# The chunk scan of an SSD layer in two halves traced one step apart, with TensorE in program order in the group loop

## The chip, the cores and the metric

The kernel runs on one NeuronCore of a Trainium2 chip. The metric is the device time of one execution, in microseconds (us), from the first to the last instruction. Its engines each take their instructions in order: TensorE (PE, with the weight loads on PEld), VectorE (DVE), ScalarE (ACT), GpSimd (POOL) and SyncE (SP), whose queue issues nearly all DMAs. Matmuls write to PSUM banks of 128 x 512 numbers; tiles for the other engines are in SBUF.

## The reference

One inference step of two layers, a Mamba-2 SSD layer and an MLA attention layer, for a prompt of 1024 tokens and 8 samples of 8 tokens each. The change is in the SSD layer. Per group g of 8 (4 heads of 64 columns, a state of 128):

```python
proj = jnp.einsum('btd,de->bte', h, w_in)                 # z, x, B, C, dt
xbc = jax.nn.silu(causal_conv(xbc, ...))                  # x, B, C
seg = a_cs[..., :, None] - a_cs[..., None, :]             # chunks of 128 tokens
decay = jnp.where(causal, jnp.exp(jnp.where(causal, seg, 0.0)), 0.0)
cb = jnp.einsum('bclgn,bcsgn->bgcls', cc, bc)
y_diag = jnp.einsum('bgrcls,bcsgrp->bclgrp', cb[:, :, None] * decay, xdt)
states = jnp.einsum('bcsgn,bcsgrp->bcgrpn', bc, xdt * decay_end[..., None])
# S[c+1] = chunk_decay * S[c] + states[c];  y_off = (C S) * decay_in
y = (y_diag + y_off + d_skip * xs) * silu(z)
yg = yg * rsqrt(mean(yg * yg) + eps)                      # per group
out = jnp.einsum('bte,ed->btd', yg * norm_w, w_out)
```

The prompt is 8 such chunks in series. Every sample has a recurrent state of its own that is read from memory, used in y_off, updated and written back.

## The kernel before

Products in float32 are made of three products of high and low halves (`split`: a cast on ScalarE, then a subtraction on DVE or POOL). Group 0's projections come first. Then a loop over g = 0 to 6 runs the scan of group g (`ssd_scan`, a generator) beside the projections of group g + 1 (`Group.steps`): after every yield as many projection pieces are traced as the yielded weights add up to, 21 a group. A piece is 24 matmuls: 12 pieces "pj" of 128 x 384 or 128 x 320 with the convolution's input, 9 pieces "pz" of 128 x 256 for the gate z (the last of them 16 matmuls for the 64 sample rows). The last scan (g = 7) runs beside the first half of the output projection (poa); its second half (pob) and the MLA layer follow and are left as they are.

What is traced in this order is then put in order by the framework's scheduler on every engine, TensorE's too: it takes whatever it expects to be ready first. A tile's buffers are taken in turn: a tile name with two buffers lets the third tile start only when the first one's last reader is done. The PSUM banks are tr 2, pj 2, cb 1, y 2, st 1.

A step of `ssd_scan` is one chunk of 128 tokens (i = 0 to 7), the ninth (i = 8) the 64 sample rows. The names in the profile:
- trp: transposes of x and B into the tr bank; xsT, xdt, xdd and BT come from it. xdd is split into xddh and xddl.
- cb: the product of B and C in the cb bank; cbm: the same with the mask.
- M: the cumulated log decays are read by a DMA (acs_d) into M; subtraction and minimum with 0 on DVE (L575), Exp on ScalarE (L577), product with cbm on DVE (L578).
- py: M with xdt in one half of the y bank (L582), C with the split state S in the other; st: the chunk's own state.
- y: sum, times z, squares summed (L662), times the norm weight nw on POOL (L663), written to y_d.
- For the samples: four tiles s0 with 4 sample states each for two heads (256 KB, two buffers), read (L628), transposed (s0p, L631), split (sh, sl), multiplied with C into pv, which lies in the cb bank (L640), decayed on POOL (L641), sn (L644) added on DVE (L646), written (L647). x3p, x3, b3 and bb are the operands of sn, for two of the four tiles at a time. yo collects pv on ScalarE and DVE (L652, L653).
- wraw, wih, wil: a projection weight as loaded (L272) and its two halves (L129 on ScalarE, L130 on DVE); woh, wol: the halves of w_out (L703, L704), wol by turns on DVE and POOL.
- ahead of the loop `ssd_dt` turns the last columns of the projection into dt, with softplus on ScalarE, and cumulates with the matmuls dpa, dpt, acsp and decp; acs_d is written from that.

Of the kernel before, what the change touches and what calls it, by code (L numbers as in the profile page):

```python
# [405 lines left out]
class Group:  # L406
# [10 lines left out]
    def pair(self, pi, both=False):  # L417
# [3 lines left out]
        if both:  # L421
            for _ in range(3):
# [98 lines left out]
def ssd_scan(k, gr, pools):  # L521
    nc, I = k.nc, k.I
    sp, psum = pools
    g = gr.g
    S = None
    hs = slice(4 * g, 4 * g + 4)
    nw = sp.tile([128, 256], F32, tag="nw", name=f"nw{g}", bufs=1)
    nc.sync.dma_start(nw, I["ssd_norm_w"][0, 256 * g : 256 * g + 256].partition_broadcast(128))
    for i in ORDER[g]:
        t0, m = TILES[i]  # L530
        sl = slice(t0, t0 + m)
        smp = i == 8
        B, C, X0, X1 = (gr.xc[q][1][:, j] if smp else gr.xc[q][0][:, j, sl] for q in range(2) for j in range(2))
        z = gr.z[i // 5][:m, i % 5]
        tag = f"{g}_{i}"
        p = psum.tile([128, 512], F32, tag="tr", name="trp" + tag, bufs=PB["tr"])
        nc.tensor.transpose(p[:m, 0:128], X0, k.ident)
        nc.tensor.transpose(p[:m, 128:256], X1, k.ident)
        if not smp:
            nc.tensor.transpose(p[:m, 256:384], B, k.ident)  # L540
        xsT = sp.tile([128, 256], F32, tag="xsT", name="xsT" + tag, bufs=2)
        nc.scalar.copy(xsT[:m], p[:m, 0:256])
        if not smp:
            Bh, Bl = (sp.tile([128, 128], F32R, tag="BT" + x, name="BT" + x + tag, bufs=2) for x in "hl")
            split(k, Bh, Bl, p[:, 256:384])
        tk = k.tok[:m, i]

        def hb(j):
            return tk[:, j, hs].unsqueeze(2).to_broadcast([m, 4, 64])

        def v3(t):
            return t[:m].rearrange("p (h q) -> p h q", q=64)

# [20 lines left out]
        for h in range(4):  # L574
            nc.vector.tensor_scalar(M[:m, h, :m], M[:m, h, :m], tk[:, 0, 4 * g + h : 4 * g + h + 1], 0.0,  # L575
                                    op0=ALU.subtract, op1=ALU.min)
# [1316 lines left out]
```

## Time and profile before

| | |
|---|---|
| median of 3 runs | 2095.51 us (2094.92 to 2098.74) |
| profiled execution, span | 2095.4 us |
| mean granted clock of TensorE | 0.969 |
| start and group 0's projections | 0 to 133 us |
| group loop, g = 0 to 6 | 133 to 848 us, some 104 us a group |
| last scan with poa | 848 to 1017 us |
| pob | 1017 to 1125 us |
| MLA layer | 1125 to 2095 us |

The profile is of one execution. Busy time is given for each engine; for matmuls, which overlap, the busy time of a stretch is the time in which at least one was running. A row of the timeline has the start, the duration, the engine, the line and the operation, then output and operands, and in brackets how long the engine stood idle before it and what ended that. A row of the stretches has the length, the busy time (and instructions) of PE, PEld, DVE, ACT and POOL, the granted clock (1.00 is full speed), the share of DMA engines and GB/s. A row of waits has the sum, the number of times and the longest.

### The profile page before, as it was taken

The numbers are of one execution on the slowest core, as the hardware profiler recorded it, in microseconds if no ns is written. First come the engines' busy times: TensorE is split into PE (matmuls) and PEld (weight loads), VectorE is DVE, ScalarE is ACT, GpSimd is POOL, SyncE is SP. The second block draws the span as 40 slices with busy tenths as digits, with TensorE's granted clock in tenths as the row PEclk, the third lists the DMA queues.
The fourth block names the chain that finished last, engine by engine and source line by source line (L and its number), as shares of the span: only waits on it lengthen the run. The fifth ranks groups of instructions, "written<-read, shape, count | busy, mean of one in ns | idle before, by whom it ended". The sixth has DMA issues, their size and how long they took to land.

```text
span 2095.4 us, 33766 instructions
## 1 busy us (share of the span) xinstructions
PE 1948.3 (93%) x12001; PEld 1763.6 (84%) x12001; DVE 1340.1 (64%) x2838; ACT 1043.3 (50%) x2287; POOL 851.9 (41%) x1059
## 2 busy tenths in 40 slices
PE   6999999999999999789998999699999999889998
PEld 5898999899999998677787998698888888778887
DVE  4558676767676767865334314366787778776665
ACT  5455565556565656522114323234676667755552
POOL 0337564646664646744000001102343334765541
PEclk9999999999999999889999999899999989999999
DMA  4222324231324241635534342132111112464451
GB/s 144 56 59 64 111 66 115 56 114 57 105 66 115 56 115 46 208 122 192 183 124 133 124 152 63 52 108 68 48 55 52 43 37 61 133 197 131 142 152 40
DMA packets 187631, 207.61 MB, mean 99 GB/s; under 512 B 23260, under 2 KB 153064, under 8 KB 187080
## 3 DMA queue, kind: packets, MB, share of 16 engines
q1 hardware_dynamic: 182408, 185.67, 29.2%
q0 software_dynamic: 4976, 19.66, 3.0%
q8 instruction: 95, 1.56, 0.3%
q14 instruction: 72, 0.59, 0.1%
q10 hardware_dynamic: 80, 0.13, 0.0%
HBM read 152.10 MB, written 53.28 MB: 98 GB/s over the span
## 4 chain that ended last, share of the span: by engine, by line
PE 33%; DVE 9%; issue 4%; POOL 4%; DMA 3%; ACT 2%; SPq 0%; POOLq 0%; DVEq 0%; ACTq 0%
PE pq L100 5%; PE pob L100 5%; PE pj L88 4%; PE poa L100 2%; POOL kvl L1541 2%; PE pk L100 1%; PE p L100 1%; PE vp L88 1%; PE st L1246 1%; DVE tl L1260 1%; PE st L1248 1%; PE st L1247 1%; PE o L1277 1%; PE sc L1214 1%; PE kp L88 1%
## 5 line engine op out<-in xcount | busy, mean ns | idle before, releaser
L88 PE MATMUL pj<-xh,wih 128*128 128x384 f32 (+1 forms) x768 | 254.9, 336 | 10.9 <-ACT xh L235 6.6
L88 PE MATMUL pj<-xl,wih 128*128 128x384 f32 (+1 forms) x768 | 255.9, 333 | 0.0
L88 PE MATMUL pj<-xh,wil 128*128 128x384 f32 (+1 forms) x768 | 255.1, 332 | 0.0
L1260 POOL TENSOR_TENSOR tl<-P,th 128x384 fp32r<-128x384 f32 (+1 forms) x96 | 90.7, 945 | 181.0 <-ACT P L1258 138.5
L88 PEld LDWEIGHTS pj<-xh,wih 128*128 128x128 f32 x768 | 145.8, 191 | 12.5 <-ACT xh L235 7.5
L468 DVE SCALAR_TENSOR_TENSOR acc<-raw,vec,acc 128x1112 f32<-128x1112 f32 x96 | 147.0, 1535 | 11.9 <-ACT acc L465 11.1
L88 PEld LDWEIGHTS pj<-xh,wil 128*128 128x128 f32 x768 | 146.3, 190 | 0.6
L88 PEld LDWEIGHTS pj<-xl,wih 128*128 128x128 f32 x768 | 146.1, 190 | 0.5
L575 DVE TENSOR_SCALAR M<-M,tok 128x128 f32<-128x128 f32 (+1 forms) x288 | 116.6, 462 | 43.0 <-DMA M<-acs_d 35.7
L100 PE MATMUL pz<-wih,xh 128*128 128x256 f32 x504 | 143.0, 287 | 0.0
L100 PE MATMUL pz<-wil,xh 128*128 128x256 f32 (+1 forms) x504 | 142.8, 287 | 0.0
L1257 ACT ACTIVATE th<-st 128x512 fp32r<-128x512 f32 x192 | 94.1, 490 | 73.6 <-PE st L1253 54.7
L100 PE MATMUL pz<-wih,xl 128*128 128x256 f32 x448 | 128.1, 286 | 0.0
L130 DVE TENSOR_TENSOR wil<-wraw,wih 128x512 fp32r<-128x512 f32 x88 | 70.4, 802 | 65.7 <-ACT wih L129 63.1
L1541 POOL TENSOR_TENSOR kvl<-pgr,kvh 128x1024 fp32r<-128x1024 f32 x32 | 78.2, 2445 | 67.8 <-ACT kvh L1540 67.8
L100 PEld LDWEIGHTS pz<-wih,xh 128*128 128x128 f32 x504 | 96.0, 190 | 1.1
L577 ACT ACTIVATE M<-M 128x512 f32<-128x512 f32 (+1 forms) x72 | 43.8, 608 | 102.0 <-DVE M L575 101.7
L1258 ACT ACTIVATE P<-st 128x512 f32<-128x512 f32 x192 | 93.2, 486 | 0.0
L100 PEld LDWEIGHTS pz<-wil,xh 128*128 128x128 f32 (+1 forms) x504 | 92.9, 184 | 0.3
L663 POOL TENSOR_TENSOR y<-y,nw 128x256 f32<-128x256 f32 (+1 forms) x72 | 64.5, 896 | 70.2 <-ACT xD L662 69.7
L582 PEld LDWEIGHTS py<-xdt,M 128*128 128x128 f32 (+1 forms) x576 | 70.4, 192 | 19.8 <-DVE xdt L555 6.5
L100 PEld LDWEIGHTS pz<-wih,xl 128*128 128x128 f32 x448 | 85.4, 191 | 0.4
(819 smaller groups left out, 6461.6 us busy)
## 6 DMA issues: line engine op xcount, KB each, us to landing
wraw<-in_ssd_w_in SPq DMA_DIRECT2D x92, 256.0 KB
M<-acs_d SPq DMA_DIRECT2D x64, 256.0 KB
s<-in_state_ssm SPq DMA_DIRECT2D x32, 256.0 KB
y_d<-y SPq DMA_DIRECT2D x64, 128.0 KB
out_s_ssm<-s SPq DMA_DIRECT2D x32, 256.0 KB
wraw<-in_ssd_w_out SPq DMA_DIRECT2D x16, 512.0 KB
q_d<-qt SPq DMA_DIRECT2D x32, 192.0 KB
qp<-q_d SPq DMA_DIRECT2D x8, 768.0 KB
```

Of the source, the lines that this page charges most:

```text
L88: nc.tensor.matmul(out, a, b, start=(i == 0), stop=(i == n - 1))
L100: nc.tensor.matmul(o, a, b, start=(j == 0), stop=(j == len(ops) - 1))
L130: (eng or nc.vector).tensor_tensor(lo, src, hi.bitcast(F32), op=ALU.subtract)
L468: nc.vector.scalar_tensor_tensor(acc, raw[:, j : j + n], k.convw[j][:, blk : blk + 1], acc, op0=ALU.mult, op1=ALU.add)
L575: nc.vector.tensor_scalar(M[:m, h, :m], M[:m, h, :m], tk[:, 0, 4 * g + h : 4 * g + h + 1], 0.0, op0=ALU.subtract, op1=ALU.min)
L577: nc.scalar.activation(M[:m, :, :m], M[:m, :, :m], AF.Exp)
L582: nc.tensor.matmul(py[:m, h * 64 : h * 64 + 64], M[:m, h, :m], xdt[:m, h * 64 : h * 64 + 64], start=True, stop=True)
L663: nc.gpsimd.tensor_tensor(y[:m], y[:m], nw[:m], op=ALU.mult)
L1257: nc.scalar.activation(th[:, :n], ps[:, :n], AF.Exp, scale=SCALE)
L1258: nc.scalar.activation(P[:, :n], ps[:, :n], AF.Exp, scale=SCALE)
L1260: eng.tensor_tensor(tl[:, :n], P[:, :n], th[:, :n].bitcast(F32), op=ALU.subtract)
L1541: nc.gpsimd.tensor_tensor(rl, raw, rh.bitcast(F32), op=ALU.subtract)
```

## The change

1. The generator `ssd_scan` becomes a class `Scan`. A chunk is done by `front(i)` (read of M, trp, xdt, xdd, cb, the decay in M) and `back(i)` (st, py, the update of S, the splits of the new S and of the next chunk's C, y). front(i + 1) is traced ahead of back(i), with yields after each: 17 yields of 15/17 for the chunks and five of 6/5 for the samples. The samples' work is cut into `turn_state(n)` (read of s0, s0p, split), `use_state(n)` (pv, decay, sn, write) and `triples(q)` (x3p to bb); turn_state(n + 1) is traced ahead of use_state(n). Buffers: M 3 (2 before), xddh and xddl 2 (1), xsT 1 (2), y 1 (2); s0 stays at 2.
2. The loop over the groups stands under `tc.manual_schedule` for TensorE: its instructions keep the order in which they are traced. The other engines are scheduled as before, and so are the start and the last scan.
3. The decay is four Relu on ScalarE (scale -1, bias the row's own value), then Exp with scale -1, in place of the four subtractions on DVE.
4. The norm weight is multiplied into w_out: woh is made by ScalarE with it as a scale, wol by a scalar_tensor_tensor on DVE for all 16 blocks. The product on POOL and the DMA of nw are gone.
5. The Silu of both column pairs of a group stand behind the second pair.

TensorE has 11581 matmul instructions in both; DVE goes from 2840 to 2560, ACT from 2123 to 2439 (288 Relu, and 78 table loads in place of 50), POOL from 1064 to 984, SP from 843 to 835.

```diff
         xs = self.ap.tile([128, 2, NB * NT], F32, tag=f"xs{pi}", name=f"xs{g}{pi}", bufs=1)
-        nc.scalar.activation(acc[:, :, :SEQ], acc[:, :, :SEQ], AF.Silu)
-        nc.scalar.activation(xs.rearrange("p a (b w) -> p a b w", w=NT),
-                             bass_window(acc, SEQ + 3, NT + 3, NT), AF.Silu)
         self.xc.append((acc, xs))
         if pi:
+            for acc, xs in self.xc:
+                nc.scalar.activation(acc[:, :, :SEQ], acc[:, :, :SEQ], AF.Silu)
+                nc.scalar.activation(xs.rearrange("p a (b w) -> p a b w", w=NT),
+                                     bass_window(acc, SEQ + 3, NT + 3, NT), AF.Silu)
...
-def ssd_scan(k, gr, pools):
...
+class Scan:
...
+    def front(self, i):
...
+        M = c.M = self.tile([128, 4, 128], "M", "M" + tag, 3)
+        nc.sync.dma_start(M[:m, :, :m], (k.acss_d[hs] if smp else k.acs_d[i, hs]).partition_broadcast(m))
+        p = self.bank("tr", "trp" + tag)
+        nc.tensor.transpose(p[:m, 0:128], c.X0, k.ident)
+        nc.tensor.transpose(p[:m, 128:256], c.X1, k.ident)
...
+        xsT = self.tile([128, 256], "xsT", "xsT" + tag, 1)
         nc.scalar.copy(xsT[:m], p[:m, 0:256])
...
+        xdt = c.xdt = self.tile([128, 256], "xdt", "xdt" + tag, 2)
+        nc.vector.tensor_tensor(c.v3(xdt), c.v3(p[:, 0:256]), c.hb(1), op=ALU.mult)
...
+            c.Bh, c.Bl = (self.tile([128, 128], "BT" + x, "BT" + x + tag, 2, F32R) for x in "hl")
+            split(k, c.Bh, c.Bl, p[:, 256:384])
+            c.dh, c.dl = (self.tile([128, 256], "xdd" + x, "xdd" + x + tag, 2, F32R) for x in "hl")
+            xdd = self.tile([128, 256], "xdd", "xdd" + tag, 1)
+            nc.gpsimd.tensor_tensor(c.v3(xdd), c.v3(xsT), c.hb(2), op=ALU.mult)
+            split(k, c.dh, c.dl, xdd, nc.gpsimd)
...
+        pc = self.bank("cb", "cb" + tag)
+        nc.tensor.matmul(pc[:m, :m], c.B, c.C, start=True, stop=True)
+        cbm = self.tile([128, 128], "cbm", "cbm" + tag, 1)
         nc.vector.tensor_tensor(cbm[:m, :m], pc[:m, :m], (k.masks if smp else k.masku)[:m, :m], op=ALU.mult)
-        M = sp.tile([128, 4, 128], F32, tag="M", name="M" + tag, bufs=2)
-        nc.sync.dma_start(M[:m, :, :m], (k.acss_d[hs] if smp else k.acs_d[i, hs]).partition_broadcast(m))
         for h in range(4):
-            nc.vector.tensor_scalar(M[:m, h, :m], M[:m, h, :m], tk[:, 0, 4 * g + h : 4 * g + h + 1], 0.0,
-                                    op0=ALU.subtract, op1=ALU.min)
-        nc.scalar.activation(M[:m, :, :m], M[:m, :, :m], AF.Exp)
+            nc.scalar.activation(M[:m, h, :m], M[:m, h, :m], AF.Relu, bias=tk[:, 0, 4 * g + h : 4 * g + h + 1], scale=-1.0)
+        nc.scalar.activation(M[:m, :, :m], M[:m, :, :m], AF.Exp, scale=-1.0)
         nc.vector.tensor_tensor(M[:m, :, :m], M[:m, :, :m],
                                 cbm[:m, :m].unsqueeze(1).to_broadcast([m, 4, m]), op=ALU.mult)
-        py = psum.tile([128, 512], F32, tag="y", name="py" + tag, bufs=PB["y"])
+        return c
...
+    def back(self, c, nxt):
+        k, nc, i, hs, tag = self.k, self.k.nc, c.i, self.hs, c.tag
+        ps = self.bank("st", "st" + tag)
+        py = self.bank("y", "py" + tag)
+        mm3(nc, ps[:, :256], [(c.Bh, c.dh), (c.Bh, c.dl), (c.Bl, c.dh)])
+        self.within(c, py)
+        S, S2 = self.S, self.tile([128, 256], "S", f"S{self.g}_{i + 1}", 2)
+        if S is None:
+            nc.vector.tensor_copy(S2, ps[:, :256])
         else:
+            Sh, Sl = self.split_S
+            mm3(nc, py[:, 256:], [(c.Ch, Sh), (c.Ch, Sl), (c.Cl, Sh)])
+            nc.gpsimd.tensor_tensor(S2.rearrange("p (h q) -> p h q", q=64), S.rearrange("p (h q) -> p h q", q=64),
+                                    k.decp[:, hs, i : i + 1].to_broadcast([128, 4, 64]), op=ALU.mult)
+            nc.vector.tensor_tensor(S2, S2, ps[:, :256], op=ALU.add)
+        self.S = S2
+        if i < 7:
+            Sh, Sl = self.split_S = [self.tile([128, 256], "S" + x, "S" + x + tag, 1, F32R) for x in "hl"]
+            split(k, Sh, Sl, S2, nc.gpsimd)
+            nxt.Ch, nxt.Cl = (self.tile([128, 128], "C" + x, "C" + x + tag, 1, F32R) for x in "hl")
+            split(k, nxt.Ch, nxt.Cl, nxt.C, nc.gpsimd)
+        self.out(c, py, py[:, 256:] if i else None)
+
...
+    def out(self, c, py, off):
...
         nc.vector.tensor_tensor(y[:m], y[:m], z, op=ALU.mult)
-        nc.scalar.activation(xD[:m], y[:m], AF.Square, accum_out=k.yssq[:m, i, g : g + 1])
-        nc.gpsimd.tensor_tensor(y[:m], y[:m], nw[:m], op=ALU.mult)
-        nc.sync.dma_start(k.y_d[sl, 256 * g : 256 * g + 256], y[:m])
+        nc.scalar.activation(c.xD[:m], y[:m], AF.Square, accum_out=k.yssq[:m, i, g : g + 1])
+        nc.sync.dma_start(k.y_d[c.sl, 256 * g : 256 * g + 256], y[:m])
...
+    def triples(self, c, q):
+        k, nc, tag, hs = self.k, self.k.nc, c.tag, self.hs
+        p = self.bank("tr", f"x3p{tag}{q}")
+        xr = self.tile([128, 4, 128], "M", f"xr3{tag}{q}", 3)[:, :3, :96]
...
+        x3 = c.x3 = self.tile([96, 256], "xddh", f"x3{tag}{q}", 2, F32R)
...
+    def turn_state(self, c, n):
+        k, nc, tag = self.k, self.k.nc, c.tag
+        q, pr = divmod(n, 2)
+        h0 = 4 * self.g + 2 * pr
+        bs = slice(4 * q, 4 * q + 4)
+        s0 = self.tile([128, 4, 128], "s0", f"s0{tag}{n}", 2)
+        nc.sync.dma_start(s0, k.I["state_ssm"][0, bs, h0 : h0 + 2].rearrange("b h p n -> (h p) b n"))
+        pt = self.bank("tr", f"s0p{tag}{n}")
+        for b in range(4):
+            nc.tensor.transpose(pt[:, b * 128 : b * 128 + 128], s0[:, b], k.ident)
+        sh, sl = (self.tile([128, 512], "s" + x, f"s{x}{tag}{n}", 1, F32R) for x in "hl")
+        split(k, sh, sl, pt)
+        return n, s0, sh, sl
+
+    def use_state(self, c, pv, n, s0, sh, sl):
...
+        for b in range(4):
+            sb = slice(b * 128, b * 128 + 128)
+            x = [(pv[:32, o], k.cblk[q][:, b, :32], sl[:, sb]), (pv[:64, o], k.cblk[q][:, b], sh[:, sb])]
+            for j, (a, u, v) in enumerate(x if b else x[::-1]):
+                nc.tensor.matmul(a, u, v, start=(b + j == 0), stop=(b == 3 and j == 1))
+        nc.gpsimd.tensor_tensor(s0, s0, k.decs[:, h0 // 2, bs].unsqueeze(2).to_broadcast([128, 4, 128]), op=ALU.mult)
+        pt = self.bank("st", f"sn{tag}{n}")
+        nc.tensor.matmul(pt, c.x3[:, pr * 128 : pr * 128 + 128], c.bb.rearrange("p b n -> p (b n)"),
+                         start=True, stop=True)
+        nc.vector.tensor_tensor(s0, s0, pt.rearrange("p (b n) -> p b n", b=4), op=ALU.add)
+        nc.sync.dma_start(k.O["s_ssm"][0, bs, h0 : h0 + 2].rearrange("b h p n -> (h p) b n"), s0)
+
+    def samples(self, c):
...
+        held = self.turn_state(c, 0)
+        self.last_state()
+        yield SW / 5
+        self.triples(c, 0)
+        pv = self.bank("cb", "pv" + c.tag)
+        for n in range(4):
+            nxt = self.turn_state(c, n + 1) if n < 3 else None
+            if n == 3:
+                py = self.bank("y", "py" + c.tag)
+                self.within(c, py)
+            yield SW / 5
+            self.use_state(c, pv, *held)
+            held = nxt
+            if n == 1:
+                self.triples(c, 1)
+        yo = self.tile([128, 256], "fo", "yo" + c.tag, 1)
+        for q in range(2):
+            r, s = slice(32 * q, 32 * q + 32), slice(256 * q, 256 * q + 256)
+            nc.scalar.copy(yo[r], pv[32:64, s])
+            nc.vector.tensor_tensor(yo[r], yo[r], pv[:32, s], op=ALU.add)
+        self.out(c, py, yo)
+
+
+def ssd_scan(k, gr, pools):
+    sc = Scan(k, gr, pools)
+    w = (21 - SW) / 17
+    c = sc.front(0)
+    yield w
+    for i in range(8):
+        nxt = sc.front(i + 1)
+        yield w
+        sc.back(c, nxt)
+        c = nxt
+        yield w
+    yield from sc.samples(c)
...
         nc.sync.dma_start(raw, wo[kk * 128 : kk * 128 + 128])
-        nc.scalar.copy(hi, raw)
-        (nc.vector if kk % 2 else nc.gpsimd).tensor_tensor(lo, raw, hi.bitcast(F32), op=ALU.subtract)
+        nw = k.ssdn[:, kk : kk + 1]
+        nc.scalar.activation(hi, raw, AF.Copy, scale=nw)
+        nc.vector.scalar_tensor_tensor(lo, raw, nw, hi.bitcast(F32), op0=ALU.mult, op1=ALU.subtract)
         ws.append((hi, lo))
...
-        for g in range(G - 1):
-            nx = Group(k, g + 1, pools)
-            steps = nx.steps()
-            done = 0
...
+        with tc.manual_schedule(engines={nc.tensor.engine}):
+            for g in range(G - 1):
+                nx = Group(k, g + 1, pools)
+                steps = nx.steps()
+                done = 0
+                w = 0
+                for x in ssd_scan(k, gr, (sp, psum)):
+                    w += x
+                    while done < int(w + 0.01):
+                        next(steps, None)
+                        done += 1
+                for _ in steps:
+                    pass
+                gr = nx
```

TensorE, the samples' state 1 in the scan of group 1, before (sn_810 is its sn, pz the gate's projection):

```order
L640 MATMUL pv_8_3501<-sl_810_3578,cblk_1092 32x128
L640 MATMUL pv_8_3501<-sh_810_3577,cblk_1092 64x128
L644 MATMUL sn_810_3590<-bb_80_3518,x_80_3512 128x512
L100 MATMUL pz<-wil,xh 128x256
L100 MATMUL pz<-wih,xl 128x256
L100 MATMUL pz<-wih,xh 128x256
```

The same place in the changed kernel (sn_81 is the sn of state 1, s0p_83 the transposes of state 3, whose tile s_83 takes the buffer of state 1):

```order
L676 MATMUL pv_8_3532<-sl_81_3541,cblk_1092 32x128
L676 MATMUL pv_8_3532<-sh_81_3540,cblk_1092 64x128
L679 MATMUL sn_81_3631<-bb_80_3530,x_80_3524 128x512
L637 MATMUL x3p_81_3635<-ident,xr_81_3636 96x128 x3
L661 MATMUL s0p_83_3655<-ident,s_83_3653 128x128 x4
L100 MATMUL pz<-wih,xh 128x256
L100 MATMUL pz<-wil,xh 128x256
L100 MATMUL pz<-wih,xl 128x256
```

The gate pieces that followed sn now follow s0p of the state that reuses the buffer; with states 0 and 2 it is the same, without x3p between.

TensorE from the end of group 0's scan to the first chunk of group 1, before (trp_0 are that chunk's transposes):

```order
L640 MATMUL pv_8_2149<-sl_801_2295,cblk_1093 32x128
L640 MATMUL pv_8_2149<-sh_801_2294,cblk_1093 64x128
L537 MATMUL trp_0_2451<-ident,acc_1541 128x128
L538 MATMUL trp_0_2451<-ident,acc_1541 128x128
L540 MATMUL trp_0_2451<-ident,acc_1148 128x128
L88 MATMUL pj<-xl,wih 128x384
L88 MATMUL pj<-xh,wil 128x384
L88 MATMUL pj<-xh,wih 128x384
```

And changed:

```order
L676 MATMUL pv_8_2191<-sh_83_2319,cblk_1093 64x128
L679 MATMUL sn_83_2421<-bb_81_2310,x_81_2304 128x512
L547 MATMUL trp_0_2442<-ident,acc_1545 128x128
L548 MATMUL trp_0_2442<-ident,acc_1545 128x128
L550 MATMUL trp_0_2442<-ident,acc_1163 128x128
L568 MATMUL cb_0_2462<-acc_1163 128x128
L547 MATMUL trp_1_2474<-ident,acc_1545 128x128
L548 MATMUL trp_1_2474<-ident,acc_1545 128x128
L550 MATMUL trp_1_2474<-ident,acc_1163 128x128
L568 MATMUL cb_1_2494<-acc_1163 128x128
L88 MATMUL pj<-xh,wih 128x384
```

The scan's last matmuls and the next scan's first two chunks' transposes and cb now stand without a projection matmul between them. What SP issues there, in the changed kernel (at the same place of the next group):

```order
L682 DMA out_s_ssm<-s_82_3584 128x4x128
L658 DMA s_80_4812<-in_state_ssm 128x4x128
L272 DMA wraw<-in_ssd_w_in 128x4x128
L682 DMA out_s_ssm<-s_83_3653 128x4x128
L272 DMA wraw<-in_ssd_w_in 128x4x128
L658 DMA s_81_4874<-in_state_ssm 128x4x128
```

The weight loads stand behind the writes of this group's last states and a read for the next group.

TensorE at the start of the loop, before (dpa, dpt: the sums of the log decays):

```order
L88 MATMUL pj<-xl,wih 128x384
L357 MATMUL dpa<-dta,masku 128x256
L358 MATMUL dpa<-dta,masks 128x32
L357 MATMUL dpt<-dta,ones 128x256
L358 MATMUL dpt<-dta,blks 128x32
L88 MATMUL pj<-xh,wil 128x384
L88 MATMUL pj<-xh,wih 128x384
```

And changed, where group 0's gate pieces come directly before:

```order
L100 MATMUL pz<-zdh_761,xh 128x288
L357 MATMUL dpa<-dta,masku 128x256
L358 MATMUL dpa<-dta,masks 128x32
L357 MATMUL dpt<-dta,ones 128x256
L358 MATMUL dpt<-dta,blks 128x32
L380 MATMUL acsp<-ident,acs 128x128 x2
L381 MATMUL acsp<-ident,acs 32x64
L88 MATMUL decp<-ra,selp 128x128 x2
L547 MATMUL trp_0_1101<-ident,acc_554 128x128
L548 MATMUL trp_0_1101<-ident,acc_554 128x128
L550 MATMUL trp_0_1101<-ident,acc_258 128x128
L568 MATMUL cb_0_1121<-acc_258 128x128
```

The pj matmuls of group 1 that stood ahead of dpa, between dpt and acsp and behind decp come after cb of chunk 1; then follow st and py of chunk 0.

More of the change, by code (lines that the diff above doesn't have):

```diff
@@ L530, in ssd_scan @@
         t0, m = TILES[i]
+        smp = i == 8
         sl = slice(t0, t0 + m)
[L532 to L538, printed above, removed]
+        c.i, c.m, c.sl, c.tag = i, m, sl, f"{g}_{i}"
@@ L539, in ssd_scan @@
+        tag = c.tag
+        c.B, c.C, c.X0, c.X1 = (gr.xc[q][1][:, j] if smp else gr.xc[q][0][:, j, sl] for q in range(2) for j in range(2))
+        M = c.M = self.tile([128, 4, 128], "M", "M" + tag, 3)
[3 more added lines that the diff above has]
+        nc.tensor.transpose(p[:m, 128:256], c.X1, k.ident)
         if not smp:
-            nc.tensor.transpose(p[:m, 256:384], B, k.ident)
@@ L541, in ssd_scan @@
-        xsT = sp.tile([128, 256], F32, tag="xsT", name="xsT" + tag, bufs=2)
+            nc.tensor.transpose(p[:m, 256:384], c.B, k.ident)
+        xsT = self.tile([128, 256], "xsT", "xsT" + tag, 1)
         nc.scalar.copy(xsT[:m], p[:m, 0:256])
-        if not smp:
[L544 to L549, printed above, removed]
```

181 lines of the change are left out of this document (62 added, 119 removed).

## The prediction

> **What bounds the kernel now.** I read the page's totals and the clock first. The runs lie between 2094.92 and 2098.74 us; that is 0.18%, so 0.2% (4 us) is about what a measurement of this kernel can tell from no change. The profiled execution spans 2095.4 us, as long as the median run (2095.51), so I sum against 2095.4.
>
> ```profile
> PE 1948.3 (93%) x12001; PEld 1763.6 (84%) x12001; DVE 1340.1 (64%) x2838; ACT 1043.3 (50%) x2287; POOL 851.9 (41%) x1059
> core 0: 2095.4 us, clock 0.969
> ```
>
> PE is the bound. The table of stretches, cut at the stages that the change touches, says by how much: in the group loop (133 to 848 us) PE works 686.98 of 715 us, and in the last scan (848 to 1017) 146.98 of 169. So 28.0 and 22.0 us of idle PE are all that a better order could take out here, plus the price of a slow clock.
>
> ```profile
> 133.00:848.00 715.00, 686.98 (x4962) 662.69 (x4961) 524.76 (x1040) 404.72 (x920) 429.78 (x635) 0.99 0.30 86
> 848.00:1017.00 169.00, 146.98 (x730) 118.53 (x728) 111.13 (x179) 53.61 (x118) 82.57 (x86) 0.91 0.53 174
> ```
>
> The waits of PE in the group loop say for what it idles: mostly that the operands of a chunk (xdd, xdt, S, M) are not ready when their matmuls are due, and seldom for a sample state.
>
> ```profile
> PE st L88 <- ACT xddh L129: 10.6, 13, 1.8
> PE py L582 <- DVE xdt L555: 5.2, 6, 1.6
> PE py L88 <- POOL Sl L130: 3.3, 6, 0.9
> PE s0p L631 <- DMA s<-in_state_ssm: 2.2, 3, 1.1
> ```
>
> **Part 1, the chunks in two halves: a gain.** With the preparation (front) a step ahead of the use (back), two to three projection pieces lie between them in TensorE's order; the rows above should go. PE's work stays as it is. I take 22 of the 28.0 us; the rest is group ends, which part 3 prices. A stall costs more than its length: after the 1.17 us wait for xddh at 475.6 the granted clock is 0.50 for 6.80 us.
>
> ```profile
> 476.79 0.39 PE L88 MATMUL st<-xddh,BTh 128*128 128x256 f32 x1 [1.17 <-ACT xddh L129]
> 478.60:485.40 6.80, 6.80 (x32) 6.67 (x30) 3.51 (x7) 4.46 (x12) 3.91 (x7) 0.50 0.30 93
> 584.40:587.80 3.40, 3.40 (x17) 3.40 (x16) 2.04 (x4) 3.06 (x6) 1.49 (x3) 0.50 0.00 0
> ```
>
> At half clock such a stretch loses 3.4 us; the second stretch of this kind loses 1.7, so 5 us go too: together **-27** (bounds -33 and -10). [...]
>
> **Part 2, the sample states: the large loss.** In the new order of TensorE the transposes of state 2 (s0p_82) stand right behind the sn matmul of state 0, and those of state 3 behind sn and three x3p transposes of state 1. The tile s0 has two buffers. So state 2 can be read only once state 0 has been updated and written out, and PE, in order, waits the whole round trip. It showed before, for one buffer (sn, add, write, then the read into the same buffer):
>
> ```profile
> 420.02 0.40 PE L644 MATMUL sn<-bb,x 96*128 96x512 f32 x1
> 421.19 0.68 DVE L646 TENSOR_TENSOR s<-s,sn 128x512 f32<-128x512 f32 x1
> 421.89 0.39 SPq L647 DMA_DIRECT2D out_s_ssm<-s  x1
> 424.25 0.38 SPq L628 DMA_DIRECT2D s<-in_state_ssm  x1
> 427.89 0.60 PE L631 MATMUL s0p<-ident,s 128*128 128x128 f32 x4
> 420.40:427.90 7.50, 7.50 (x67) 7.33 (x66) 3.93 (x10) 2.51 (x9) 1.04 (x1) 1.00 0.48 140
> ```
>
> From the end of sn to the issue of the read took 424.25 - 420.42 = 3.83 us. The last row is PE's work between sn and s0p: 7.50 of 7.50 us, all gate projections. That is the cover, and in the new order nothing of it is left. The flight of the read itself is seen where PE did wait for it:
>
> ```profile
> 428.05 0.37 SPq L628 DMA_DIRECT2D s<-in_state_ssm  x1
> 432.00 0.66 PE L631 MATMUL s0p<-ident,s 128*128 128x128 f32 x4 [0.34 <-DMA s<-in_state_ssm]
> 844.19 0.37 SPq L628 DMA_DIRECT2D s<-in_state_ssm  x1
> 846.81 0.44 PE L631 MATMUL s0p<-ident,s 128*128 128x128 f32 x2 [0.72 <-DMA s<-in_state_ssm]
> ```
>
> 3.95 and 2.62 us. So one round trip is 6.45 to 7.8 us. I take 6.6, near the lower end, since while PE stands little else is moved. Two stalls in each of the 7 scans of the loop: 14 x 6.6 = **+92** (bounds 77, if some 1 us of each is covered, and 109). Behind PE's wait stand the next gate piece, then pv and sn, so nothing of PE goes on; the other engines catch up, which doesn't shorten PE's list.
>
> After a long stall the clock is at half for 3.4 us, as in the MLA part:
>
> ```profile
> 1437.50:1441.00 3.50, 0.01 (x1) 0.00 (x0) 3.12 (x6) 0.80 (x3) 2.92 (x3) 1.00 0.78 231
> 1441.10:1444.50 3.40, 3.40 (x10) 2.84 (x11) 1.87 (x6) 1.03 (x3) 3.34 (x5) 0.51 0.38 112
> 1444.50:1447.90 3.40, 3.40 (x19) 2.94 (x18) 2.96 (x11) 1.37 (x3) 0.92 (x2) 0.99 0.02 5
> ```
>
> A stretch of 3.40 us at 0.51 does the work of 1.7 us: 14 x 1.7 = **+24** (bounds 0, and 48 if each takes 6.8 us as above).
>
> **Part 3, the group boundary: a loss.** In TensorE's order sn of state 3, trp_0, cb_0, trp_1 and cb_1 now stand in a row; before, 21 matmuls lay between trp_0 and the next step of the scan. cb_0 needs the bank of pv, so the second yo add; on DVE that stands behind a wil split whose weights are loaded by SP, and SP issues this load behind the read of the next group's first state, which waits for the write of state 2. cb_1 needs the same single bank back, so cbm_0, which stands behind another wil split whose load SP issues after the write of state 3. Price of one load with its split:
>
> ```profile
> 224.37 0.37 SPq L272 DMA_DIRECT2D wraw<-in_ssd_w_in  x1
> 227.37 0.62 ACT L129 CAST wih<-wraw 128x512 fp32r<-128x512 f32 x1 [2.35 <-DMA wraw<-in_ssd_w_in]
> 228.02 0.69 DVE L130 TENSOR_TENSOR wil<-wraw,wih 128x512 fp32r<-128x512 f32 x1 [1.55 <-ACT wih L129]
> ```
>
> 4.34 us from issue to the end of the split. Counted from the end of sn of state 2: 3.83 (as in part 2) to the state's read, 0.4 to the load, 4.3, and an add of 0.4: cb_0 at about 9, while PE has there only the last 16 gate matmuls and pv, an estimated 3 to 5 us by the pace of part 2's row (67 matmuls in 7.50 us). cb_1 follows some 2 us later. So 6 boundaries in the loop at 6 us: **+36** (bounds 18 and 48), and the clock as above, 6 x 1.8 = **+11** (0 to 20).
>
> **Part 4, the start of the loop: a loss.** dpa, acsp, decp, trp and cb follow the last piece of group 0's projection in a row, then 24 pj matmuls, st_0 and py_0. Before, PE filled the same time with pj:
>
> ```profile
> 116.90:124.40 7.50, 7.07 (x41) 6.75 (x39) 1.67 (x5) 6.88 (x10) 0.41 (x1) 1.00 0.00 0
> 124.48 0.70 PE L357 MATMUL dpa<-dta,masku 128*128 128x256 f32 x2 [0.51 <-DVE dta L351]
> 133.70:145.50 11.80, 11.80 (x79) 11.71 (x77) 9.99 (x24) 6.78 (x19) 8.00 (x14) 1.00 0.55 147
> 140.21 2.18 DVE L575 TENSOR_SCALAR M<-M,tok 128x128 f32<-128x128 f32 x8 [0.77 <-DMA M<-acs_d]
> ```
>
> The softplus chain on ScalarE keeps dpa at about 124.5, and M comes from memory at 140.2; with its ReLUs, Exp and product (part 5) py_0 can start at about 143. From 116.9 to 143 are 26 us, and PE has then about 9 us of work: 24 pj at 11.80/79 = 0.15 to 0.17 us each (4), the dt, transpose and cb matmuls (4) and st_0 (0.5). 26 - 9 = **+17** (bounds 12 and 25); two stalls, so **+3** for the clock (0 to 7).
>
> **Part 5, decay on ScalarE, and w_out.** Four DVE operations of 0.445 us become four Relu; the nearest rows on ScalarE for 128 x 128 are 0.281 and 0.294.
>
> ```profile
> L575 DVE TENSOR_SCALAR M<-M,tok 128x128 f32<-128x128 f32 x200 | 77.4, 445 | 31.7 <-DMA M<-acs_d 31.6
> L129 ACT CAST BTh<-trp 128x128 fp32r<-128x128 f32 x48 | 13.5, 281 | 0.0
> L577 ACT ACT_TABLE_LOAD x19 | 24.4, 1283 | 1.7 <-DMA M<-acs_d 1.3
> ```
>
> ScalarE gets 36 x 0.29 = 10.4 us a group and, by the built program, 4 more table loads, 5.1 us: 404.72/715 busy becomes about 0.71. It stays off the path, hidden by the projection pieces between front and back; without that cover each chunk would pay (rival C). The removed nw product on POOL and its DMAs were off the path: 0. In the last scan, which is still scheduled freely, DVE is the bound in the middle:
>
> ```profile
> 870.00:890.00 20.00, 13.01 (x66) 10.72 (x67) 19.85 (x35) 9.71 (x21) 16.21 (x18) 0.83 0.52 170
> L575 DVE TENSOR_SCALAR M<-M,tok 128x128 f32<-128x128 f32 x24 | 14.9, 673 | 0.1
> L704 DVE TENSOR_TENSOR wol<-wraw,woh 128x1024 fp32r<-128x1024 f32 x4 | 8.3, 2069 | 0.0
> ```
>
> DVE loses 36 x 0.67 = 24 us there and takes over some four wol that POOL had, 8.3: net -16, of which I take **-10** (bounds -22, all of the stage's idle, and +5 if the moved order hurts).
>
> **The rivals.** *A, only the state round trips count* (20%): if waits of PE overlap the boundary, and the slow clock is shorter, as 848 to 1017 shows 0.91 with 22 us of idle: 2095 + 85 (14 x 6.1) + 17 - 27 + 5 to 15 (clock) = about 2180. *B, the other side* (4%): the round trip has passed when PE gets to s0p, and the chunk waits vanish: 2095 - 27 - 10 = 2058. It needs at least 6.45 us of matmuls between sn_80 and s0p_82; from 6.45 us of cover on the change wins. For it speaks that all that waited in the table of waits is moved apart, against it that PE's order is fixed and has none there. *C, ScalarE or its table loads become late* (8%): if py waits for M 0.6 to 1 us in each of the 63 chunks, +38 to +63: about 2290. *D, the change doesn't do what it says* (2%): other engines' order still spoils the early front, the 22 us stay and the rest is as forecast: 2263.
>
> **How the numbers follow.** 2095 + 92 + 24 + 36 + 11 + 17 + 3 - 27 - 10 = 2241 us, with 66%. The low end, 2175, takes in A; the high end, 2295, the upper bounds of half of the terms and C and D. Faster by over 0.2%: B, 4%, of which 1% falls to within 0.2%. Slower: 96%.
>
> **What would show it.** Right: in PE's waits, s0p behind the state's read with 14 long waits of 5 to 8 us, two at a time in each group; cb behind yo and cbm with some 3 to 6 us at six boundaries; a stall of about 7 us before dpa and one of about 10 before py_0; half clock behind each; st behind xddh and py behind xdt gone from the list; a group of some 120 us instead of 104. Wrong: s0p without waits, or groups of 104 us or less; then part 2 has fallen and with it the forecast.

## The result, and the profile after

The changed kernel takes 2311.74 us (2307.37 to 2313.36, 4 runs), the kernel before 2095.97 in the same comparison: a ratio of 1.102, with a 95% interval of 1.1004 to 1.1035. Slower was forecast, but by 146 us instead of 216; the time lies 17 us above the range. The profiled execution spans 2311.6 us. Its totals and its clock:

```profile
PE 2006.0 (87%) x12001; PEld 1824.5 (79%) x12001; DVE 1240.1 (54%) x2558; ACT 1166.7 (50%) x2603; POOL 806.7 (35%) x979
core 0: 2311.6 us, clock 0.926
```

The trace has 12001 matmul records in both kernels (420 more than the program's 11581 instructions). They keep PE busy for 58 us longer, and the granted clock is 0.926 instead of 0.969: some of the loss is work at half clock, the rest is idle. The table of stretches, first of before and then of after: the loop (from 116.9 us to the last gate matmul), the last scan, and the MLA layer.

```profile
116.90:846.10 729.20, 701.38 (x5039) 675.83 (x5037) 528.49 (x1050) 414.41 (x934) 430.47 (x636) 0.99 0.30 84
846.10:1016.70 170.60, 147.87 (x739) 119.35 (x739) 111.92 (x182) 54.50 (x121) 83.03 (x86) 0.91 0.52 173
1123.00:2095.40 972.40, 901.06 (x5162) 797.65 (x5160) 614.52 (x1492) 507.72 (x1115) 313.40 (x286) 0.96 0.31 95
```

```profile
116.90:1056.80 939.90, 757.47 (x5057) 735.21 (x5058) 441.51 (x790) 529.15 (x1227) 408.79 (x575) 0.89 0.22 65
1056.80:1225.30 168.50, 145.46 (x727) 118.94 (x724) 96.63 (x159) 62.92 (x144) 59.51 (x67) 0.90 0.52 171
1332.60:2311.60 979.00, 903.26 (x5162) 798.59 (x5160) 616.34 (x1492) 507.82 (x1115) 312.84 (x286) 0.96 0.30 94
```

The loop is 210.7 us longer: 56.1 us of longer matmuls and 154.6 us of idle PE (182.4 instead of 27.8). The last scan gained 2 us, the MLA layer, whose code is the same, lost 6.6. PE's waits in the loop say what the 182 us are:

```profile
PE s0p L661 <- DMA s<-in_state_ssm: 84.6, 13, 7.3
PE cb L568 <- DVE yo L711: 34.7, 6, 6.0
PE ctp L476 <- POOL ct L464: 25.5, 7, 3.9
PE dpa L357 <- DVE dta L351: 7.6, 1, 7.6
PE pj L88 <- ACT raw L456: 7.1, 7, 1.0
PE s0p L661 <- DVE sl L130: 6.0, 1, 6.0
PE py L581 <- DVE M L574: 5.8, 1, 5.8
PE sn L679 <- POOL bb L649: 5.0, 7, 2.1
PE cb L568 <- DVE cbm L570: 4.0, 5, 0.8
```

Nothing of st for xddh or of py for xdt and Sl is left. In their place stand 14 waits for a sample state (13 named with the read, the 14th with the split sl; 90.6 us), six at the group boundary, two at the start, as forecast, and 7 waits of ctp, which were not. One round trip in the timeline of after, with all its links:

```profile
363.33 0.49 PE L679 MATMUL sn<-bb,x 96*128 96x512 f32 x1 [1.58 <-POOL bb L649]
363.86 0.69 DVE L681 TENSOR_TENSOR s<-s,sn 128x512 f32<-128x512 f32 x1 [1.70 <-PE sn L679]
364.58 0.38 SPq L682 DMA_DIRECT2D out_s_ssm<-s  x1
366.89 0.39 SPq L658 DMA_DIRECT2D s<-in_state_ssm  x1
369.76 1.08 PE L661 MATMUL s0p<-ident,s 128*128 128x128 f32 x4 [5.93 <-DMA s<-in_state_ssm]
```

Write to read 2.31 us, read to s0p 2.87: 5.93 us of idle PE, and 6.86 for state 3. The granted clock behind four stalls (ctp, state 2, state 3, boundary) in the same group:

```profile
339.20:346.00 6.80, 5.65 (x27) 5.49 (x27) 5.38 (x7) 1.64 (x4) 5.26 (x8) 0.50 0.36 99
366.50:373.30 6.80, 3.54 (x17) 3.57 (x18) 0.69 (x1) 1.49 (x2) 1.04 (x1) 0.50 0.13 39
380.10:387.00 6.90, 4.19 (x20) 4.22 (x21) 0.00 (x0) 2.46 (x4) 1.04 (x1) 0.51 0.13 38
400.60:407.50 6.90, 5.12 (x17) 4.75 (x18) 5.62 (x13) 3.10 (x9) 5.10 (x6) 0.51 0.57 155
```

Each is 6.8 us at half clock, partly spent in the stall itself; the second number, PE's busy time, halved, is what it costs by an estimate from the clock of 0.50 and 0.51: 1.8 to 2.8 us.

### The profile page after: what moved, and what is told of

Read it like the earlier page. It is cut to its first block, busy times and chain, and to the rows that moved or that the text cites. A ratio compares the mean times of both kernels' runs of the same rounds, so it can differ in the third digit from the quotient of the medians.

```text
span 2311.6 us, 33496 instructions
## 1 busy us (share of the span) xinstructions
PE 2006.0 (87%) x12001; PEld 1824.5 (79%) x12001; DVE 1240.1 (54%) x2558; ACT 1166.7 (50%) x2603; POOL 806.7 (35%) x979
## 5 line engine op out<-in xcount | busy, mean ns | idle before, releaser
L100 PE MATMUL pz<-wih,xh 128*128 128x256 f32 x504 | 163.6, 328 | 0.0
L572 ACT ACTIVATE M<-M,tok 128x128 f32<-128x128 f32 (+1 forms) x288 | 90.6, 385 | 111.7 <-DMA M<-acs_d 104.9
L100 PE MATMUL pz<-wih,xl 128*128 128x256 f32 x448 | 143.0, 319 | 0.0
L100 PEld LDWEIGHTS pz<-wih,xh 128*128 128x128 f32 x504 | 115.3, 229 | 0.9
L100 PEld LDWEIGHTS pz<-wil,xh 128*128 128x128 f32 (+1 forms) x504 | 111.4, 221 | 0.0
L563 POOL TENSOR_TENSOR xdd<-xsT,tok 128x256 f32<-128x256 f32 x64 | 43.3, 677 | 189.3 <-ACT xsT L552 185.9
L661 PE MATMUL s0p<-ident,s 128*128 128x128 f32 x128 | 26.9, 348 | 92.4 <-DMA s<-in_state_ssm 86.3
L509 ACT COPY z<-pz 128x256 f32<-128x256 f32 x64 | 23.5, 367 | 158.5 <-PE pz L100 143.7
L100 PEld LDWEIGHTS pz<-wih,xl 128*128 128x128 f32 x448 | 103.5, 231 | 0.0
L681 DVE TENSOR_TENSOR s<-s,sn 128x512 f32<-128x512 f32 x32 | 21.9, 685 | 137.9 <-PE sn L679 137.9
```

The lines of the kernel that those rows point to most:

```text
L100: nc.tensor.matmul(o, a, b, start=(j == 0), stop=(j == len(ops) - 1))
L509: nc.scalar.copy(z[:m, i % 5], p[:m, :256])
L563: nc.gpsimd.tensor_tensor(c.v3(xdd), c.v3(xsT), c.hb(2), op=ALU.mult)
L572: nc.scalar.activation(M[:m, h, :m], M[:m, h, :m], AF.Relu, bias=tk[:, 0, 4 * g + h : 4 * g + h + 1], scale=-1.0)
L661: nc.tensor.transpose(pt[:, b * 128 : b * 128 + 128], s0[:, b], k.ident)
```

## The experiments

Two theories are held against each other. The first: the loss comes from the places where TensorE's traced order has no cover (states, boundary, ctp, start). The second: the new halves, their buffers and ScalarE's additional work are slow in themselves. "Before" ran again beside each set, at 2099.8 to 2102.3 us.

**Without the reads of states 2 and 3.** Their steps take tiles that are already there:

```diff
-        s0 = self.tile([128, 4, 128], "s0", f"s0{tag}{n}", 2)
-        nc.sync.dma_start(s0, ...)
+        if n < 2:
+            s0 = self.tile([128, 4, 128], "s0", f"s0{tag}{n}", 2)
+            nc.sync.dma_start(s0, ...)
+            self.s0s = [s0] if n == 0 else [self.s0s[0], s0]
+        else:
+            s0 = self.s0s[3 - n]
```

> The changed kernel, but the sample states 2 and 3 are not read: their step takes the tile of state 1 and of state 0 again, which are in SBUF by then. All that TensorE does is the same, in the same order. Theory (TensorE stands for the round trip of the two state buffers): the 14 waits of s0p for the state's read (86.3 us, and 6.0 put down to the split sl) go, and with them up to 14 x 3.4 us of lost work at half clock: 2311.7 - 90 = 2221 at the most, 2174 if all of the clock comes back. Rival (the waits are only the place where TensorE meets a delay that comes from the other engines, and something else is late next, bb, the split or cb): less than 45 us of gain, above 2265.

2222.64 us, 89 less than the changed kernel and 2 us above the theory's range. The waits for the read are gone; the waits in the samples' part that took over part of their place:

```profile
PE pv L680 <- ACT sh L129: 11.9, 7, 2.2
PE s0p L665 <- DVE cblk L695: 10.0, 7, 1.5
```

So the round trip is the largest single cause among those tried, and its full price (90.6 us of waits and the clock) is not all had back, since 22 us of new waits come up behind it.

**ctp later, and projection pieces at the boundary**, each alone on the changed kernel:

```diff
         if pi:
             ...
-            self.conv_out()
             ...
             if i == 0:            # Group.gates, first gate piece
+                self.conv_out()
```

> The changed kernel with one step traced later: the four transposes ctp of the convolution's last rows come behind the first gate piece of the group instead of right behind the last projection piece, whose copies they need. Theory: their 7 waits of 3.8 us (25.5 us) go, and 7 x 3.4 us at half clock at the most: 2262 to 2286. Rival (the wait moves to the gate piece behind, whose bank or weights come as late): above 2300.

```diff
-                w = 0
+                w = 2
+                for _ in range(2):
+                    next(steps, None)
+                    done += 1
                 for x in ssd_scan(k, gr, (sp, psum)):
-                    w += x
+                    w += x * 19 / 21
```

> The changed kernel with two of the 21 projection pieces of every group traced ahead of the scan's first front, so that 48 pj matmuls (8 us) stand between sn of the last state and cb of the next group; the other steps share the 19 that are left. Theory: the 6 waits of cb for yo (34.7 us) and most of the wait of py for the first M (5.8) go, with up to 7 x 3.4 us at half clock: 2247 to 2275. Rival (taken from the cover of other steps, so that st or py wait there): above 2290. The state round trips stay as they are.

2286.01 and 2241.27 us: 26 and 70 less. In the first the wait for ct is gone, but in the profiled run the loop is only 21 us shorter: 12 us of idle and 9 of busy time, as the wait for sl grew from 6.0 to 12.1 us and one of x3p came up (4.7). So the time fell by as much as was expected at the least, and part of the wait moved on. It is a stall that the transposes have because they stand directly behind the projection whose last copies they need, and these copies in their turn stand behind two weight casts on ScalarE and an update of S on POOL (the changed kernel's timeline):

```profile
337.39 1.14 ACT L129 CAST wih<-wraw 128x512 fp32r<-128x512 f32 x2
338.70 0.23 ACT L456 COPY raw<-pj 128x64 f32<-128x64 f32 x1
339.15 1.00 POOL L596 TENSOR_TENSOR S<-S,decp 128x256 f32<-128x256 f32 x1
340.10 0.20 POOL L464 COPY ct<-raw 128x24 f32<-128x24 f32 x1
340.35 0.41 PE L476 MATMUL ctp<-ident,ct 128*27 128x128 f32 x1 [3.86 <-POOL ct L464]
```

The second gave more than was expected of it. Its stretch of the loop shows why (868.90 us instead of 939.90): 45 us less idle, the wait of dpa among it, for which the two pieces of the first group now stand ready, and 26 us less busy time, at a granted clock of 0.91 instead of 0.89. PE works 97 us at half clock in it instead of 144; half of the difference, 23.5 us, is an estimate of what that brings of the 26 us. The wait of ctp grew (31.3 us instead of 25.5).

```profile
116.90:985.80 868.90, 731.36 (x5047) 712.76 (x5046) 451.49 (x789) 507.55 (x1211) 391.52 (x575) 0.91 0.24 70
```

**All mended at once**, nothing left out: s0 in three buffers (M in two for it), state 3 behind the next gate piece, both edits above, and pv in a bank of y.

> The changed kernel with the four places mended and nothing left out: three buffers for s0 (M has two for it) and the transposes of state 3 behind the next gate piece; ctp behind the first gate piece; two projection pieces ahead of the first front; pv in a bank of y, so that cb doesn't wait for yo. Theory (the losses add up): 2311.7 - 89 (state round trips, as without the reads) - 26 (ctp) - 70 (boundary) = 2127, or 2095 to 2130 with what the slow clock gives back more when all the long stalls are gone. Rival (the stalls hid one another, and ScalarE and DVE are late next): above 2150.

2105.10 us, a ratio to before of 1.0030 (1.0001 to 1.0059). The losses add up, and the slow clock gives back some more (the granted clock is 0.98 in its loop, 0.89 in the changed kernel's): the first theory holds for 207 of the 216 us. But mended it is only as fast as before. PE still idles for 35.6 us in its loop, 8.0 of them before the first py. And it holds the norm weight in w_out, which alone on the kernel before gives 2064.17 us beside the same runs of before (below): 41 us less than the mended kernel.

**The fixed order on the old code**: only `manual_schedule` around the old loop.

> The kernel before with one part alone: its TensorE in the order in which the old ssd_scan traces it. Theory (the halves one step apart are what makes a fixed order bearable): with preparation and use of a chunk in one step TensorE stands in each of the 56 chunks for the chain from trp over M to py, 5 to 8 us and the slow clock behind it, and for every state in turn: 2500 to 2800. Rival (the fixed order is the whole loss, however the chunks are traced): 2280 to 2350, as the changed kernel.

2511.57 us, with these waits in the loop:

```profile
PE py L582 <- DVE M L578: 93.5, 29, 11.3
PE py L582 <- DVE xdt L555: 74.3, 34, 3.8
```

So the halves do what they are made for: a fixed order costs 410 us without them and 167 us in the new code, whose other parts are in that figure too (next run), and these two waits all but vanish.

**The new code without the fixed order** (`manual_schedule` taken away):

> The changed kernel without the fixed order: TensorE is scheduled in the group loop as before. Theory (nearly all of the loss comes from TensorE's order): s0p, cb, ctp and the start find gate or projection matmuls ahead of them again, 2065 to 2110. Rival (the cut into two halves itself, the single buffers of xsT and y, and ScalarE's Relu and table loads are to blame for a part): above 2130, with waits of py for M and of st for xddh in every chunk.

2144.35 us, a ratio of 1.0211 (1.018 to 1.0242). Neither theory alone: 167 of the 216 us come from the order, but the scheduler, free to fill every gap, still loses 44 us with the new code. That is the rival's time, but not with the waits that it named; PE's longest are:

```profile
PE py L88 <- POOL Sl L130: 13.5, 12, 2.1
PE pj L88 <- ACT raw L453: 7.6, 5, 2.1
PE ctp L476 <- POOL ct L464: 7.5, 7, 1.2
PE pv L676 <- ACT sh L129: 7.2, 9, 1.7
```

Three kernels undo one part each of this version: xsT and y in two buffers again and M in two; the first pair's Silu back in its place; the decay back on DVE.

> The changed code with TensorE scheduled freely (2144 us), and buffers given back: xsT and y two each as before, M two. Theory (the single buffers make the chunk's preparation wait for the last use on POOL and for the write of y): 2085 to 2120, with shorter waits of py for Sl. Rival (the buffers don't bind, the extra comes from the order in which the other engines take the halves): 2135 to 2155.

> The changed code with TensorE scheduled freely (2144 us), and the Silu of the first column pair back behind that pair. Theory (two pairs' Silu in a row, some 8 us of ScalarE, hold up raw, z and sh, for which pj, ctp and pv wait there): 2115 to 2130. Rival (they are as late in two parts): 2138 to 2150.

> The changed code with TensorE scheduled freely (2144 us), and the decay back on DVE. Theory (with two halves in flight ScalarE is the late engine: Relu and 28 more table loads, some 100 us of it in the loop): 2105 to 2125, with shorter waits for sh, raw and z. Rival (as on the kernel before, where Relu alone changed little): 2138 to 2150.

2108.47, 2141.54 and 2119.11 us. The old buffers are worth 36 us (M goes from three to two in that kernel too): the waits for Sl and sh are no longer among the long ones. The decay on ScalarE costs 25 us where two halves are in flight: with it on DVE the waits for Sl (8.0 us instead of 13.5) and raw fall, though the one for sh grows (10.7 instead of 7.2). The Silu costs nothing that can be told. Whether the two that count overlap or add up was not tried. Nor was what the norm weight brings inside the new code; if it is the 36 us that it brings alone (below), the other parts lose some 80 us there, not 44.

**Single parts on the kernel before.** The decay by Relu alone:

> The kernel before with one part alone: the four subtractions of the decay on DVE become Relu on ScalarE and Exp with scale -1; order and buffers as before. Theory of the prediction (ScalarE has room, DVE is relieved in the last scan): 2085 to 2101 where before is at 2096 to 2101. Rival (the table loads and Relu make ScalarE's results late, which is what is left of the loss in the freely scheduled version): 2110 to 2140, with longer waits of st for xddh, py for M or Sl.

2092.81 us, a ratio of 0.9979 (0.9948 to 1.001): no difference that can be told, the loop 3.6 us longer and the last scan 6.7 shorter in the profiled run. The norm weight in w_out alone (the fold):

```diff
-        nc.gpsimd.tensor_tensor(y[:m], y[:m], nw[:m], op=ALU.mult)
...
-        nc.scalar.copy(hi, raw)
-        (nc.vector if kk % 2 else nc.gpsimd).tensor_tensor(lo, raw, hi.bitcast(F32), op=ALU.subtract)
+        nc.scalar.activation(hi, raw, AF.Copy, scale=k.ssdn[:, kk : kk + 1])
+        nc.vector.scalar_tensor_tensor(lo, raw, k.ssdn[:, kk : kk + 1], hi.bitcast(F32), op0=ALU.mult, op1=ALU.subtract)
```

> The kernel before with one part alone: the norm weight is multiplied into w_out, all 16 wol on DVE, the product with nw on POOL and its DMAs gone. Theory: the product was off the path; in the last scan DVE gets some four wol of 2 us that POOL had, and that stage is bound by DVE: 0 to +8 us. Rival (POOL's product held the squares, y and so the buffers): 10 us or more faster.

2064.17 us, a ratio of 0.9838 (0.978 to 0.9896): 36 us faster than before (by the interval 22 to 46), against the theory; the rival had said 10 or more. The loop, which holds nothing of w_out, is where it shows in the profiled execution: 704.70 us instead of 729.20, with 15.5 us of idle PE instead of 27.8. The other 12 us are busy time of PE; 3.4 of them are half clock that is gone (3.4 us of it in the loop instead of 10.2), the rest is not explained.

```profile
116.90:821.60 704.70, 689.18 (x5035) 672.38 (x5033) 512.70 (x1049) 413.93 (x935) 387.13 (x574) 1.00 0.30 85
```

Before's own timeline shows two queues just ahead of the wait for xddh that the prediction quoted:

```profile
472.74 1.26 POOL L663 TENSOR_TENSOR y<-y,nw 128x256 f32<-128x256 f32 x1 [2.33 <-ACT xD L662]
473.96 0.46 POOL L130 TENSOR_TENSOR Cl<-acc,Ch 128x128 fp32r<-128x128 f32 x1
474.39 0.73 POOL L130 TENSOR_TENSOR Sl<-S,Sh 128x256 fp32r<-128x256 f32 x1
475.09 0.61 POOL L558 TENSOR_TENSOR xdd<-xsT,tok 128x256 f32<-128x256 f32 x1
475.81 0.63 ACT L577 ACTIVATE M<-M 128x512 f32<-128x512 f32 x1 [1.84 <-DVE M L575]
476.35 0.39 ACT L129 CAST xddh<-xdd 128x256 fp32r<-128x256 f32 x1
```

The product waits 2.33 us for the squares of y on ScalarE and then takes 1.26; C, S and xdd of the next chunk are queued behind it on POOL, xddh behind xdd, and st behind xddh, which PE reached 1.17 us too early. But on ScalarE xddh also stands behind the Exp of M, which waited 1.84 us for DVE's subtraction, and that ended within 0.1 us of xdd. So in this place POOL alone would not have let st start earlier in the same order of ScalarE; the six waits of xddh over 1.1 us that look like it have both queues in them.

That POOL's counts is borne out by the run with the decay by Relu, in which Exp no longer waits for DVE: st then waits for xddl on POOL (12.7 us instead of 2.7; for xddh 7.4 instead of 10.6). And in the run with the norm weight folded, Exp waiting for DVE stands ahead of xddh in seven of the eight waits that are left (5.1 us in all). The gain of the product's going is measured; its way through POOL's queue is argued.

The groups of POOL in before's loop have the sum: 54.5 us of products, and 65.0 us for which the queue stood.

```profile
L663 POOL TENSOR_TENSOR y<-y,nw 128x256 f32<-128x256 f32 (+1 forms) x62 | 54.5, 880 | 65.0 <-ACT xD L662 64.9
```

Both parts together on the kernel before:

> The kernel before with two parts together: the norm weight in w_out and the decay by Relu on ScalarE; TensorE scheduled freely, chunks as before. Theory (the two relieve different engines, POOL and DVE, and add up): the fold's gain of about 35 us and the last scan's 7: 2050 to 2062 where the fold alone gave 2064. Rival (ScalarE's later xddh takes back what the fold gave): 2066 or more.

2074.08 us, a ratio of 0.9867 (0.9839 to 0.9895). That is the rival's time: the Relu adds nothing to the fold that can be told (the intervals overlap). Whether xddh on ScalarE is why is not shown: its waits are not longer (4.5 us against 5.1), those for xddl on POOL are (9.2 against 0.3). The version with the fold alone beats both kernels.

## Why the prediction was wrong in size

The direction, the state round trips and the places of the other stalls that were named were right. The steps that failed are terms of the sum: the list of waits left out 38 us, the slow clock was put at +33 us and cost 56, and the last scan and what follows it were put some 8 us each too low.

**State round trips (part 2): right.** 14 waits, two a scan, 90.6 us against 92; 5.7 to 7.3 us each against 6.6.

**Boundary (part 3): the place and the size right, the chain only in part, and so partly by luck.** Six waits of cb for yo, 34.7 us, and 4.0 for cbm, against 36. In the second group boundary SP issues the next state's read, then the load, then wil and yo follow, as was counted; but ScalarE was later than that.

```profile
393.21 1.28 ACT L572 ACTIVATE M<-M,tok 128x128 f32<-128x128 f32 x4 [3.92 <-DMA M<-acs_d]
393.89 0.37 SPq L658 DMA_DIRECT2D s<-in_state_ssm  x1
396.02 0.37 SPq L272 DMA_DIRECT2D wraw<-in_ssd_w_in  x1
399.65 0.62 ACT L129 CAST wih<-wraw 128x512 fp32r<-128x512 f32 x1
400.31 0.69 DVE L130 TENSOR_TENSOR wil<-wraw,wih 128x512 fp32r<-128x512 f32 x1
400.61 0.36 ACT L710 COPY yo<-pv 32x256 f32<-32x256 f32 x1
401.03 0.41 DVE L711 TENSOR_TENSOR yo<-yo,pv 32x256 f32<-32x256 f32 x1
401.59 0.77 PE L568 MATMUL cb<-acc 128*128 128x128 f32 x2 [6.00 <-DVE yo L711]
```

From the Relu of M, which waited 3.92 us for its read, ScalarE works without a gap to the second copy of yo: four Relu, Exp, a table load, Silu, casts and copies. The cast wih has no gap before it, so it did not wait for its load. By the 4.34 us that the prediction took for a load with its split, wil would have ended at 400.36; it ended at 401.00, within 0.03 us of ScalarE's copy. In the other five boundaries it is the same, 4.98 us from the load to the end of wil and no gap before wih. So the chain through SP would have ended some 0.6 us earlier, and the one that ended last is ScalarE's queue with the decay in it.

**Start (part 4): right**, 7.6 + 5.8 = 13.4 us against 17; the stall before py is 5.8 us, not the 10 or so that were named.

**What was not in the sum: 38 us of waits.** ctp for ct (25.5), pj for raw (7.1) and sn for bb (5.0). In ctp, the one of them that was moved, the cause is that of the others, a step traced directly behind what it needs; for raw and bb that is argued. The prediction looked for such places at the state, the boundary and the start, and not at the end of the convolution.

**The slow clock (parts 2 to 4): its places right, the term mis-sized.** The forecast was 24 + 11 + 3 - 5 = +33 us; PE's busy time in the loop rose by 56.1. The half-clock time there is 215 us instead of 10, and 144 us of it have PE at work: at a clock of 0.50 an estimated 72 us lost, some 2.5 us for each of the 29 stalls of 2.4 us or more, not 1.7. The step at fault took the 3.4 us stretch of the MLA part for the rule and the 6.8 us one for the upper bound; in the loop 6.8 us was the usual length (21 of 29 stretches). In the MLA part the stall ended (1441.0) as the stretch began (1441.1), so PE worked all through it; in the loop 27 of the 29 stalls reached into the stretch, and these 27 stretches lasted 6.8 us or more (last section). That busy time did not rise by the whole 67 us (72 less the 5 of before) goes with fewer changes between projection matmuls and others (680 in the loop before, 280 after); that this is the cause is argued, not shown.

**Part 1: right for the order that was forecast, with a wrong sentence on the stalls before.** The waits for xddh, xdt and Sl did vanish: 27.8 us of idle against the 22 that were taken. But the sentence that the nw product on POOL was off the path was wrong: taken out of the kernel before alone, with its DMAs, it brings 36 us. The row that the prediction shows names ScalarE as the releaser of st; the product is two links behind that, in POOL's queue. This error did not make the forecast too low: what the product is worth under the fixed order is not shown.

**Part 5: the last scan gave 2 us, not 10.** DVE's busy time in it fell by 15.3 us, as counted, but PE's waits there changed their names rather than their sum. That nothing of ScalarE's load shows on the path was wrong too: in the freely scheduled version the decay on ScalarE is worth 25 us, and in the changed kernel ScalarE's queue is the chain that ends last at the six boundaries. What the decay alone costs there was not tried.

**The MLA layer** was taken at 0 and lost 6.6 us: its instructions are the same, but its first projections and the sample part wait differently (4.1 us for hh, 4.8 for the gate's product). In the other kernels of this study, whose MLA layer is the same too, it took between 967 and 979 us, so 6.6 us are within what the same code shows. Why was not tried.

The sum as measured: 90.6 + 38.7 + 13.4 + 37.6 (missed) + 2.1 (small waits) - 27.8 (idle before) + 56.1 (busy) - 2.1 (last scan) + 7.6 (pob and MLA) = 216 us. Of the 70 us by which the forecast fell short, about 31 are idle PE, 23 the clock, 8 each the last scan and what follows it.

## What to carry to other kernels

A fixed order on an engine that stands until the operand of its next instruction is there (PE stood 5.93 us before s0p, with gate matmuls traced behind it) has to be read at every seam, not only at those that the change talks about: for each instruction that uses another engine's or a DMA's result, count the work that stands between it and what starts that result, and give it at least the length of the chain. Behind a wait in the profile look up the queue of the engine that ended it, who stood ahead there and what that one waited for, and go on until one chain is clearly the last: an operation "off the path" that waits in a queue (here the product with nw, 2.33 us for the squares of y) holds up all that is queued behind it. And a change of several parts is worth taking apart: one part of this one, alone, made the kernel 1.6% faster, under a whole that made it 10% slower.

## What the runs showed of the hardware

In the changed kernel's loop half clock followed all 29 stalls of PE of 2.4 us or more. Of the 29 stretches 21 last 6.8 us, five 10.2, two 3.4, and the one behind dpa 13.7. They begin 1.6 to 5.2 us after PE fell idle (363.8 to 366.5, 395.6 to 400.6).

The two stretches of 3.4 us stand behind stalls that had ended before the stretch began (at 208.8 and 1004.7, half clock from 209.5 and 1004.8). The other 27 stalls reached into the stretch: behind state 2 PE worked 0.14 us of the first 3.4 (366.5 to 369.9) and all of the next (369.9 to 373.3), at the boundary 1.62 us of the first 3.4 (400.6 to 404.0) and all of the rest (404.0 to 407.5).

In the kernel before, half clock came behind two short waits: 1.17 us, ended at 476.8, with half clock from 478.6 for 6.8 us, and 1.42 us, ended at 582.8, with half clock from 584.4 for 3.4 us. It did not come behind waits of 1.64 and 1.77 us in the same loop, which ended at 188.7 and 789.6: the granted clock is 1.00 from 186 to 195 and from 787 to 797. So neither the length of a wait nor its end alone gives the price of the slow clock in these runs; what sets the start and the length of a stretch is not shown.
